# Two heads' score products queued as one run, and the merge's first products as one run behind the z projection, in a two-layer encoder

## The chip, the cores and the metric

The kernel runs on one core of one Trainium2 chip. The metric is device time in microseconds (us); lower is better.

## What is computed

Two layers over 256 tokens of width 1024. In each layer the normalised tokens `h` are projected once; the slices of the projection feed a gated delta rule with 8 heads (branch a) and a differential softmax attention with 8 heads (branch b). Cut to what matters here:

```python
proj = h @ w_in[l]
(q_a, k_a, v_a, ab_a, z_a, q_b, k_b, v_b, z_b, gate_a, gate_b) = jnp.split(proj, SPLIT_IDX, axis=-1)
y_a = gated_delta_branch(q_a, k_a, v_a, ab_a, z_a, ...)      # short convolutions, a triangular solve, chunks
s = jnp.einsum('nbhqd,nbhkd->nbhqk', q_blk, k)               # branch b: two score maps n for each head
p = jax.nn.softmax(s, axis=-1)
a = p[0] - lam * p[1]
o = jnp.einsum('bhqk,bhkd->bhqd', a, v)
y_b = rmsnorm(o, subln_w) * (1.0 - lambda_init) * jax.nn.silu(z_b)
merged = sigmoid(gate_a) * (y_a @ w_pa[l]) + sigmoid(gate_b) * (y_b @ w_pb[l])
x = x + merged @ w_out[l]
```

## The kernel before, in words

**Projections.** Each weight block of 1024 x 512 arrives in four loads of 256 rows (`raw`), and each load is split in two parts that together carry the float32 value: ScalarE writes `hi` (L230), VectorE writes `lo` (L232). A projection is then three products for each of the eight row blocks and each of the two token tiles m: hi by hi, lo by hi, hi by lo (L244 to L246). `hi` and `lo` have two buffers each, so the split of load kp+2 waits until the products of load kp have read it. In the program's names, `pp_zb000` and `pp_zb001` are the two accumulators (m = 0 and 1) of projection zb, layer 0, first half, and `lo_zb002` is the third load's low part of that projection; the first digit of a name is the layer, and for heads the second is the head. Order of the projections in a layer: k, v_b, q, q and k of branch b (`qk`), v, then zb (two halves), za (two halves), and the gates gb and ga around the merges with `w_pb` and `w_pa`.

**PSUM.** Eight banks: four under the tag `p` (two accumulators of the running projection and two more, which the score products of a head use), two under `c` (the turned blocks of the convolutions, `ctv` among them, and all products of the delta rule), two under `m` (turned blocks of q and k, `qkt`; a head's turned weights, `at`; its output, `av`).

**A head of branch b** (`head`, L829 to L871) is four score products on 64 of the 128 rows of the array each, for two query tiles and the two maps n = 1, 0 in turn (L839); then VectorE takes maxima (`mx`, L846), ScalarE exponentials (`es`, L848), VectorE the combination of the maps (`cc` L851 and L852, `es` L856), TensorE turns the result (`at`, L859), ScalarE copies it, TensorE multiplies by v (`av`, L865). Heads stand between the halves of the z projections in the program, and a scheduler orders the instructions of each engine: it takes them by their place in the program, as soon as it holds them ready and their buffers free by its own estimate of durations. Instructions written under `tc.high_priority` go ahead of others; `behind(x)` keeps an instruction after x on its engine; `keep_in_program_order` keeps a product behind the one written before it.

**What runs beside the heads.** VectorE solves the triangular systems of the delta rule by substitution: 31 steps of two instructions, `fstmp` (L670) and `X` (L671), each of which needs the one before it (`substitute(0, 31)`, written before the v convolutions). It also does the four taps of each block of the v convolution (`cvv`, L527), its SiLU (`thv`, L536), and the copy of the turned blocks out of PSUM (`vtm` from `ctv`, L547), and the rotary part of q and k (`r`, `stg`, L448 to L451). ScalarE has the tanh of the convolutions (L531), the exponentials, the splits and the PSUM copies.

**The merge of the solved blocks** (`merges`) begins with 64 products of 32 x 32 for each of two groups (`y64p`, L723). The first group's products may start behind row block 5 of the second half of za (`mark["done", 5]`), the second group's and the rest follow.

Of the kernel before, what the change touches and what calls it, by code (L numbers as in the profile page):

```python
# [17 lines left out]
P = 128  # L18
DM = 1024
KT = DM // P  # L20
SEQ = 256
NM = SEQ // P
# [6 lines left out]
HP = None  # L29
# [20 lines left out]
def hybrid_encoder(  # L50
# [19 lines left out]
    V, S, G, T = nc.vector, nc.scalar, nc.gpsimd, nc.tensor  # L70
# [18 lines left out]
    def banks2(name):  # L89
        return [ps_p.tile([P, 512], F32, tag="p", name=f"{name}{i}") for i in range(2)]  # L90

    def bank_c(name):
        return ps_c.tile([P, 512], F32, tag="c", name=name)
# [7 lines left out]
    mark = {}  # L101
# [102 lines left out]
    def behind(ins):  # L204
        return nullcontext() if ins is None else tc.issue_after(ins)
# [135 lines left out]
    for l in range(DEPTH):  # L341
# [139 lines left out]
        for m in range(NM):  # L481
            T.matmul(abq[:, m * 32 : (m + 1) * 32], abT[:, m * P : (m + 1) * P], id2,
                     start=True, stop=True)
# [213 lines left out]
        def merges(g):  # L697
# [17 lines left out]

            order = [(c, j4, mm, d) for c, j4 in every for mm in range(2) for d in range(2)]
            order.sort(key=lambda k: k != (0, 0, 1, 1))
            first = mark["done", 5] if g == 0 else None
            for n_, (c, j4, mm, d) in enumerate(order):
                b0, b1 = srcdst(d, mm)  # L720
                co = 32 * (b0 % 2)
# [104 lines left out]
        s_all = small.tile([P, NH, 2, NM], F32, tag="s_all", name=f"s_all{l}")  # L826
        ssb = small.tile([P, NM, NH], F32, tag="ssb", name=f"ssb{l}")
        ob = e4(f"ob{l}", "eo")
        def head(h):  # L829
            es = work.tile([P, 2, NM, SEQ], F32, tag="w4a", name=f"es{l}{h}", bufs=2)  # L830
            mx = small.tile([P, 2, NM], F32, tag="mx", name=f"mx{l}{h}")


            sp = banks2(f"sc{l}{h}")
            for qt in range(NM):
                for n in (1, 0):
                    rows = slice(64 * n, 64 * n + 64)
                    with nullcontext() if n else tc.high_priority(offset=HP):
                        mm = T.matmul(sp[n][:, qt * SEQ : (qt + 1) * SEQ],  # L839
                                      qkT[h // 4][rows, 0, h % 4, qt * P : (qt + 1) * P],  # L840
                                      qkT[h // 4][rows, 1, h % 4, :], start=True, stop=True)
                    if qt or not n:
                        tc.keep_in_program_order(mm)
            for n in range(2):
                spv = sp[n].rearrange("p (q k) -> p q k", q=NM)
                V.tensor_reduce(mx[:, n, :], spv, AX.X, ALU.max, negate=True)  # L846
# [69 lines left out]
        qk_part(1, 0)  # L916
        conv("v", C_VA, None, 1)
        qk_part(1, 1)
        head(0)
        z_part(zb, C_ZB, "zb", 0)  # L920
        head(1)
        z_part(zb, C_ZB, "zb", 1)
        head(2)
        head(3)
        z_part(za, C_ZA, "za", 0)
        mg = [merges(0), merges(1)]
        step(mg)
        step(mg)
        head(4)
        head(5)  # L930
        z_part(za, C_ZA, "za", 1)
        step(mg)
        head(6)
        with tc.high_priority(offset=HP):
            step(mg[:1])
        head(7)
# [141 lines left out]
```

## Time and profile before

| | |
|---|---|
| three runs | 779.36 to 779.75 us, median 779.53 |
| span of the profiled execution, first to last instruction | 777.1 us |
| what the median has beside that span | 2.4 us |
| TensorE busy | 758.2 us, 98% of the span |
| VectorE, ScalarE, GpSimd busy | 557.3, 474.9, 101.9 us |

The page gives the span of the profiled execution and no device time of its own, so the median stands for it; the 2.4 us lie before the first and behind the last instruction. In a timeline each row has the start, the time to the end of the last instruction in the row, the engine, the line, the operation, output and inputs (buffer numbers left out), and how many instructions are merged in the row. Float32 products outside the projections are two instructions each, so a head's four score products show as 8.

### The profile page before, as it was taken

How to read it: one execution, taken by the hardware profiler on the slowest of the kernel's cores; microseconds unless marked ns; L12 is line 12 of the kernel's file. 1: busy time of each engine (PE TensorE's matmuls, PEld its weight loads, DVE VectorE, ACT ScalarE, POOL GpSimd, SP SyncE). 2: the span in 40 equal slices, each digit the busy share in tenths (PEclk: the TensorE clock that was granted, in tenths of full speed). 3: DMA queues.
4: the chain of work that ended last, by engine and by line, in shares of the span. 5: the costliest groups of instructions: out<-in, count | busy, mean ns of one | idle time of the engine just before them, and what ended most of it. 6: DMA issues, size and time to landing. Idle time of an engine off the chain costs nothing.

```text
span 777.1 us, 13805 instructions
## 1 busy us (share of the span) xinstructions
PE 758.2 (98%) x5222; PEld 647.7 (83%) x5222; DVE 557.3 (72%) x1051; ACT 474.9 (61%) x1042; POOL 101.9 (13%) x137
## 2 busy tenths in 40 slices
PE   8999999999999999999999999999999999999996
PEld 4899879887778888887889888899777788888784
DVE  5686878999974635377677776989999553536782
ACT  5657776557677744564554668655577776356551
POOL 5100461100030100010010025510001110001000
PEclk9999999999999999999999999999999999999998
DMA  7752756554496644346664256755446954343631
GB/s 227 240 177 78 224 146 198 174 172 136 112 207 187 210 135 129 117 144 210 215 224 136 82 160 221 194 170 161 141 137 174 233 164 160 114 133 111 213 110 54
DMA packets 77745, 126.91 MB, mean 163 GB/s; under 512 B 19679, under 2 KB 20015, under 8 KB 77680
## 3 DMA queue, kind: packets, MB, share of 16 engines
q1 hardware_dynamic: 71038, 112.99, 48.4%
q0 software_dynamic: 3936, 9.77, 4.8%
q10 hardware_dynamic: 2706, 3.28, 1.3%
q8 instruction: 41, 0.67, 0.4%
q14 instruction: 24, 0.20, 0.1%
HBM read 121.27 MB, written 4.75 MB: 162 GB/s over the span
## 4 chain that ended last, share of the span: by engine, by line
PE 81%; DVE 7%; DMA 5%; ACT 4%; issue 2%; POOL 0%; SPq 0%; POOLq 0%; ACTq 0%; DVEq 0%
PE pp_vb L282 5%; DMA raw_q<-in_w_in_dram 3%; PE pp_qk L245 2%; PE pp_qk L246 2%; PE pp_qk L244 2%; PE pp_o L282 2%; PE pf_k L298 2%; PE pf_k L302 2%; PE pf_v L298 2%; PE pf_k L300 2%; PE pp_gb L245 2%; PE sc L839 2%; PE pp_gb L244 2%; PE pf_v L302 2%; PE pf_v L300 2%; PE av L865 2%
## 5 line engine op out<-in xcount | busy, mean ns | idle before, releaser
L245 PE MATMUL pp_qk<-lo_qk,hT 128*128 128x512 f32 x128 | 51.3, 401 | 1.0 <-DVE lo_qk L232 1.0
L246 PE MATMUL pp_qk<-hi_qk,hT 128*128 128x512 f32 x128 | 50.1, 391 | 0.0
L230 ACT CAST hi_qk<-raw_qk 128x1024 fp32r<-128x1024 f32 x32 | 33.5, 1046 | 23.6 <-PE pp_qk L246 12.6
L244 PE MATMUL pp_qk<-hi_qk,hT 128*128 128x512 f32 x128 | 46.1, 398 | 0.7 <-ACT hi_qk L230 0.7
L232 DVE TENSOR_TENSOR lo_qk<-raw_qk,hi_qk 128x1024 fp32r<-128x1024 f32 x32 | 40.2, 1257 | 7.6 <-ACT hi_qk L230 7.4
L232 DVE TENSOR_TENSOR lo_pb<-raw_pb,hi_pb 128x1024 fp32r<-128x1024 f32 x16 | 19.6, 1224 | 35.7 <-ACT hi_pb L230 35.7
L298 PE MATMUL pf_q<-hT,hi_q 128*128 128x256 f32 x128 | 36.5, 288 | 0.3 <-ACT hi_q L230 0.2
L298 PE MATMUL pf_v<-hT,hi_v 128*128 128x256 f32 x128 | 36.5, 289 | 0.0
L300 PE MATMUL pf_v<-hT,hi_v 128*128 128x256 f32 x128 | 36.2, 286 | 0.0
L300 PE MATMUL pf_q<-hT,hi_q 128*128 128x256 f32 x128 | 35.9, 284 | 0.0
L848 ACT ACTIVATE es<-sc,mx 128x256 f32<-128x256 f32 x64 | 29.8, 473 | 10.1 <-DVE mx L846 10.0
L298 PE MATMUL pf_k<-hT,hi_k 128*128 128x256 f32 x128 | 35.8, 285 | 0.0
L302 PE MATMUL pf_q<-hT,lo_q 128*128 128x256 f32 x128 | 35.7, 292 | 0.0
L300 PE MATMUL pf_k<-hT,hi_k 128*128 128x256 f32 x128 | 35.7, 283 | 0.0
L232 DVE TENSOR_TENSOR lo_gb<-raw_gb,hi_gb 128x1024 fp32r<-128x1024 f32 x16 | 19.6, 1224 | 22.2 <-ACT hi_gb L230 22.0
L232 DVE TENSOR_TENSOR lo_ga<-raw_ga,hi_ga 128x1024 fp32r<-128x1024 f32 x16 | 19.6, 1226 | 21.0 <-ACT hi_ga L230 21.0
L302 PE MATMUL pf_v<-hT,lo_v 128*128 128x256 f32 x128 | 34.6, 286 | 0.0
L302 PE MATMUL pf_k<-hT,lo_k 128*128 128x256 f32 x128 | 34.4, 285 | 0.0
L230 ACT CAST hi_pb<-raw_pb 128x1024 fp32r<-128x1024 f32 x16 | 16.8, 1049 | 25.1 <-PE pp_pb L246 24.3
L527 DVE SCALAR_TENSOR_TENSOR cvq<-pf_q,cw,cvq 128x254 f32<-128x254 f32 (+1 forms) x64 | 29.7, 476 | 1.8 <-ACT cvq L523 1.4
L527 DVE SCALAR_TENSOR_TENSOR cvv<-pf_v,cw,cvv 128x254 f32<-128x254 f32 (+1 forms) x64 | 30.2, 483 | 0.6 <-ACT cvv L523 0.5
L527 DVE SCALAR_TENSOR_TENSOR cvk<-pf_k,cw,cvk 128x254 f32<-128x254 f32 (+1 forms) x64 | 28.5, 478 | 2.0 <-ACT cvk L523 1.3
(356 smaller groups left out, 2495.5 us busy)
## 6 DMA issues: line engine op xcount, KB each, us to landing
raw_qk<-in_w_in_dram SPq DMA_DIRECT2D x32, 512.0 KB, 3.7
raw_k<-in_w_in_dram SPq DMA_DIRECT2D x16, 512.0 KB, 4.6
raw_q<-in_w_in_dram SPq DMA_DIRECT2D x16, 512.0 KB, 3.7
raw_v<-in_w_in_dram SPq DMA_DIRECT2D x16, 512.0 KB, 3.8
raw_zb<-in_w_in_dram SPq DMA_DIRECT2D x16, 512.0 KB, 3.6
raw_za<-in_w_in_dram SPq DMA_DIRECT2D x16, 512.0 KB, 3.7
raw_gb<-in_w_in_dram SPq DMA_DIRECT2D x16, 512.0 KB, 4.7
raw_o<-in_w_out_dram SPq DMA_DIRECT2D x16, 512.0 KB, 4.5
```

Of the source, the lines that this page charges most:

```text
L230: high = S.copy(hi[:, :, :n], raw[:, :, :n]).ins
L232: mark[nm, kp] = high, V.tensor_tensor(lo[:, :, :n], raw[:, :, :n], hi[:, :, :n].bitcast(F32), ALU.subtract).ins
L244: T.matmul(o, act[kt // 4][:, 0, kt % 4, ts_], hi, start=kt == 0, stop=False)
L245: T.matmul(o, act[kt // 4][:, 0, kt % 4, ts_], lo, start=False, stop=False)
L246: mark["proj"] = T.matmul(o, act[kt // 4][:, 1, kt % 4, ts_], hi, start=False, stop=kt == KT - 1).ins
L282: mark["proj"] = T.matmul(o, a_, w_, start=kt == 0 and a_ is ah and w_ is hi, stop=kt == KT - 1 and a_ is al).ins
L298: T.matmul(o, hi[:, cs], act[kt // 4][:, 0, kt % 4, :], start=first, stop=False, skip_group_check=True)
L300: T.matmul(o, hi[:, cs], act[kt // 4][:, 1, kt % 4, :], start=False, stop=False, skip_group_check=True)
L302: T.matmul(o, lo[:, cs], act[kt // 4][:, 0, kt % 4, :], start=False, stop=done, skip_group_check=True)
L527: V.scalar_tensor_tensor(ca[:, o0:o1], acc[:, b, o0 + sft : o1 + sft], cw[:, j, cb : cb + 1], ca[:, o0:o1], ALU.mult, ALU.add)
L839: mm = T.matmul(sp[n][:, qt * SEQ : (qt + 1) * SEQ], qkT[h // 4][rows, 0, h % 4, qt * P : (qt + 1) * P], qkT[h // 4][rows, 1, h % 4, :], s ...
L848: S.activation(es[:, n, qt, :], spv[:, qt, :], AF.Exp, bias=mx[:, n, qt : qt + 1], accum_out=s_all[:, h, n, qt : qt + 1])
```

## The change

`head` takes one or two heads. With two, the second head's scores go to the two banks of tag `c`, the first's to tag `p` as before; the second head's four products are written first, then the first head's, all kept in that order, and behind them the softmax and the rest of the first and then of the second (`attend`, unchanged). Heads 0 and 1 stand together ahead of the z projections (before: head 0 ahead of zb, head 1 between its halves); 2 and 3 together behind row block 3 of zb's second half, 4 and 5 together behind block 3 of za's first half, 6 alone behind block 2 of za's second half. Except for heads 0 and 1 and head 7, the first product is under high priority, which it was not before. In the merge the first group's products wait for row block 7, the last, instead of 5.

```diff
-            first = mark["done", 5] if g == 0 else None
+            first = mark["done", 7] if g == 0 else None
...
-        def head(h):
+        def head(*hs, after=None):
+            sps = [banks2(f"sc{l}{hs[0]}")] + [[bank_c(f"sc{l}{h}{i}") for i in range(2)] for h in hs[1:]]
+            lead = True
+            for h, sp in reversed(list(zip(hs, sps))):
+                for qt in range(NM):
+                    for n in (1, 0):
+                        rows = slice(64 * n, 64 * n + 64)
+                        with behind(mark["done", after] if lead and after is not None else None), \
+                                nullcontext() if lead and after is None else tc.high_priority(offset=HP):
+                            mm = T.matmul(sp[n][:, qt * SEQ : (qt + 1) * SEQ],
+                                          qkT[h // 4][rows, 0, h % 4, qt * P : (qt + 1) * P],
+                                          qkT[h // 4][rows, 1, h % 4, :], start=True, stop=True)
+                        if not lead:
+                            tc.keep_in_program_order(mm)
+                        lead = False
+            for h, sp in zip(hs, sps):
+                attend(h, sp)
...
-        head(0)
+        head(0, 1)
         z_part(zb, C_ZB, "zb", 0)
-        head(1)
         z_part(zb, C_ZB, "zb", 1)
-        head(2)
-        head(3)
+        head(2, 3, after=3)
         z_part(za, C_ZA, "za", 0)
         mg = [merges(0), merges(1)]
         step(mg)
         step(mg)
-        head(4)
-        head(5)
+        head(4, 5, after=3)
         z_part(za, C_ZA, "za", 1)
         step(mg)
-        head(6)
+        head(6, after=2)
```

**TensorE behind the last product of the `qk` projection, layer 0.** `qkt` are the last turned blocks of k, `ctv010` and `ctv012` the turned blocks of the v convolution in the two `c` banks, `sc01x` and `sc00x` the scores of heads 1 and 0. Before:

```order
L246 MATMUL pp_qk0111_1999<-hi_qk0113_2054,hT0_1_108 128x512
L839 MATMUL sc001_2101<-qkT0_0_281 128x256
L839 MATMUL sc000_2100<-qkT0_0_281 128x256
L839 MATMUL sc001_2101<-qkT0_0_281 128x256
L839 MATMUL sc000_2100<-qkT0_0_281 128x256
L244 MATMUL pp_zb000_2132<-hi_zb000_2134,hT0_0_107 128x512
```

And in the changed kernel, from the same product on:

```order
L246 MATMUL pp_qk0111_1999<-hi_qk0113_2054,hT0_1_108 128x512
L454 MATMUL qkt0011_2079<-ident_81,stg0110_2072 128x128 x4
L544 MATMUL ctv010_1968<-ident_81,thv011_1965 128x128 x2
L544 MATMUL ctv012_1992<-ident_81,thv012_1980 128x128 x2
L454 MATMUL qkt0111_2092<-ident_81,stg0111_2085 128x128 x4
L838 MATMUL sc011_2101<-qkT0_0_281 128x256
L544 MATMUL ctv012_1992<-ident_81,thv013_1989 128x128 x2
L838 MATMUL sc010_2100<-qkT0_0_281 128x256
```

Behind these stand the other six score products of the two heads, and then the first product of zb. Before, the `qkt` and `ctv` products of this list stood between the products of zb; the last of them, on `thv013`, stood behind all 48 products of zb's first half. Now all of them stand ahead of zb. The order is the same in layer 1.

**VectorE on the way to `thv013`**, the difference between before (-) and the changed kernel (+), layer 0:

```order
 L670 TENSOR_TENSOR fstmp0_347<-la0_344,X0_346 128x252
 L527 TENSOR_SCALAR cvv013_1983<-pf_v011_1829,cw0_268,cvv013_1983 128x255
-L852 TENSOR_SCALAR cc00_2112<-s_all0_348,neglam0_327,cc00_2112 128x2
 L671 TENSOR_TENSOR X0_346<-X0_346,fstmp0_347 128x14x18
-L232 TENSOR_TENSOR lo_zb002_2171<-raw_zb002_2172,hi_zb002_2170 128x1024
 L527 TENSOR_SCALAR cvv013_1983<-pf_v011_1829,cw0_268,cvv013_1983 128x255
-L856 TENSOR_SCALAR es00_2098<-es00_2098,cc00_2112 128x256 x2
 L670 TENSOR_TENSOR fstmp0_347<-la0_344,X0_346 128x255
-L232 TENSOR_TENSOR lo_zb003_2189<-raw_zb003_2190,hi_zb003_2188 128x1024
```

In the same stretch the two `mx00` and the other `cc00`, a little earlier, and `lo_zb010`, right ahead of `thv013`, also go: all of them now stand behind `thv013`, and the taps of the convolution and the substitution stay.

**VectorE behind the copy of `ctv012`**, changed kernel, layer 0:

```order
L547 TENSOR_TENSOR vtm0_331<-ctv012_1992,nrm0_334 128x2x2x128
L671 TENSOR_TENSOR X0_346<-X0_346,fstmp0_347 128x17x15
L670 TENSOR_TENSOR fstmp0_347<-la0_344,X0_346 128x252
L671 TENSOR_TENSOR X0_346<-X0_346,fstmp0_347 128x18x14
L670 TENSOR_TENSOR fstmp0_347<-la0_344,X0_346 128x247
L671 TENSOR_TENSOR X0_346<-X0_346,fstmp0_347 128x19x13
```

Seven more instructions of the substitution follow (twelve in all), then the maxima `mx00` and `mx01` of the two heads with single substitution instructions between them, `cc` and `es` of both heads in the same way, and only then `lo_zb002`. Before, maxima, combinations and low parts stood among the substitution one by one.

More of the change, by code (lines that the diff above doesn't have):

```diff
@@ L828, in hybrid_encoder, with attend @@
         ob = e4(f"ob{l}", "eo")
-        def head(h):
+        def head(*hs, after=None):
[15 more added lines that the diff above has]
+                attend(h, sp)
+        def attend(h, sp):
             es = work.tile([P, 2, NM, SEQ], F32, tag="w4a", name=f"es{l}{h}", bufs=2)
             mx = small.tile([P, 2, NM], F32, tag="mx", name=f"mx{l}{h}")
[L834 to L843, printed above, removed]
             for n in range(2):
```

## The prediction

> **What bounds the kernel now.** I read the page's busy times first, then a table by stretch: zb's first half in layer 0 and the same piece of layer 1.
>
> ```profile
> PE 758.2 (98%) x5222; PEld 647.7 (83%) x5222; DVE 557.3 (72%) x1051; ACT 474.9 (61%) x1042; POOL 101.9 (13%) x137
> 171.80:190.20 18.40, 17.95 (x90) 13.59 (x90) 17.89 (x43) 12.29 (x25) 0.00 (x0) 1.00 0.47 142
> 549.90:568.30 18.40, 17.91 (x91) 13.60 (x91) 17.89 (x43) 12.31 (x26) 0.00 (x0) 1.00 0.51 141
> ```
>
> The columns of the table are TensorE, its weight loads, VectorE, ScalarE and GpSimd busy, then the granted clock, the DMA share and GB/s. TensorE has work nearly all the time (98%): an idle microsecond of it is a microsecond of the end. But in this stretch VectorE is full as well, 17.89 of 18.40 us in either layer. So both keep pace only because their work lies side by side. What matters is which work TensorE still has while VectorE goes through taps, rotations and substitution.
>
> **First part: everything ahead of zb.** TensorE's timeline, before:
>
> ```profile
> 171.81 1.78 PE L839 MATMUL sc<-qkT 64*128 64x256 f32 x8
> 173.52 0.50 PE L244 MATMUL pp_zb<-hi_zb,hT 128*128 128x512 f32 x1
> ...
> 187.49 0.40 PE L245 MATMUL pp_zb<-lo_zb,hT 128*128 128x512 f32 x1
> 187.72 0.40 PE L246 MATMUL pp_zb<-hi_zb,hT 128*128 128x512 f32 x1
> ...
> 189.10 1.16 PE L865 MATMUL av<-vb,aT 128*128 128x128 f32 x8
> 190.10 0.38 PE L544 MATMUL ctv<-ident,thv 128*128 128x128 f32 x2
> 190.24 0.47 PE L244 MATMUL pp_zb<-hi_zb,hT 128*128 128x512 f32 x1
> ```
>
> zb's first half starts at 173.52, its second at 190.24; a product comes every 0.23 us (187.49, 187.72). In the changed kernel the last `ctv012` products, on `thv013`, stand ahead of zb. TensorE works in order, so nothing of zb starts before VectorE reaches `thv013`:
>
> ```profile
> 175.88 1.29 DVE L846 TENSOR_REDUCE mx<-sc 128x2 f32<-128x512 f32 x2
> 177.08 0.29 DVE L448 TENSOR_TENSOR r<-stg,sincos 128x128 f32<-128x128 f32 x1
> ...
> 178.54 0.69 DVE L547 TENSOR_TENSOR vtm<-ctv,nrm 128x512 f32<-128x512 f32 x1
> ...
> 180.65 1.23 DVE L232 TENSOR_TENSOR lo_zb<-raw_zb,hi_zb 128x1024 fp32r<-128x1024 f32 x1
> 181.78 0.49 DVE L527 SCALAR_TENSOR_TENSOR cvv<-pf_v,cw,cvv 128x255 f32<-128x255 f32 x1
> 182.17 0.89 DVE L856 SCALAR_TENSOR_TENSOR es<-es,cc 128x256 f32<-128x256 f32 x2
> 182.96 0.43 DVE L670 TENSOR_TENSOR fstmp<-la,X 128x255 f32<-128x255 f32 x1
> 183.30 1.23 DVE L232 TENSOR_TENSOR lo_zb<-raw_zb,hi_zb 128x1024 fp32r<-128x1024 f32 x1
> ...
> 185.29 0.43 DVE L670 TENSOR_TENSOR fstmp<-la,X 128x256 f32<-128x256 f32 x1
> 186.02 1.23 DVE L232 TENSOR_TENSOR lo_zb<-raw_zb,hi_zb 128x1024 fp32r<-128x1024 f32 x1 [0.30 <-ACT hi_zb L230]
> 187.16 0.42 DVE L536 SCALAR_TENSOR_TENSOR thv<-thv,cvv 128x256 f32<-128x256 f32 x1
> ```
>
> `thv013` is the last row, 187.16. By the changed order VectorE no longer does ahead of it: the two `mx` (175.88 to 177.08: 1.20), the two small `cc` (0.2), `lo` (180.65 to 181.78: 1.13), the two `es` (182.17 to 182.96: 0.79), `lo` again (1.13) and the third `lo` with its wait (from 185.72, the end of `fstmp`, to 187.16: 1.44). That is 5.9 us, so `thv013` starts at 181.3 and ends at 181.7. The `ctv012` products need 0.4. VectorE's copy `vtm` (0.69) then starts at 182.3, behind two substitution instructions, and ends at 183.0. Only then is the second `c` bank free for `sc010`; the first bank's copy stands ahead of the later taps and lets one score product through early. So of the run of eight, one comes alone and seven follow from 183.0. For their length:
>
> ```profile
> 195.57 0.39 PE L246 MATMUL pp_zb<-hi_zb,hT 128*128 128x512 f32 x1
> 195.89 1.13 PE L839 MATMUL sc<-qkT 64*128 64x256 f32 x8
> 196.96 0.73 PE L244 MATMUL pp_zb<-hi_zb,hT 128*128 128x512 f32 x2
> 197.53 0.60 PE L859 MATMUL at<-ident,es 128*128 128x128 f32 x4
> 196.43 0.60 PE L839 MATMUL sc<-qkT 64*128 64x256 f32 x4
> 196.65 0.38 PE L839 MATMUL sc<-qkT 64*128 64x256 f32 x2
> ```
>
> Four score products last 1.07 us (195.89 to 196.96); inside the run one more costs 0.22 (196.43 to 196.65, two instructions at once on the two halves of the rows). Seven cost 1.07 + 3 x 0.22 = 1.7, and **zb starts at 184.8 instead of 173.5**. Of these 11.3 us some 3 are work that TensorE did later before (8 `qkt`, 6 `ctv`, one head's scores); the others are waiting.
>
> The same rows price a run: from 195.57 to 197.53 there are three projection products (0.69) and four score products (0.87), together 1.56 of 1.96. So **entering and leaving costs 0.4 us**. That is what the change saves where a run goes.
>
> **Second part: zb's first half waits for VectorE again.** The first two loads' products, 24 x 0.23 = 5.5, end at 190.3. Then comes `at00`, which needs the softmax of head 0. Behind `vtm` VectorE has twelve substitution instructions in a row, each of which needs the one before:
>
> ```profile
> 195.99 0.41 DVE L671 TENSOR_TENSOR X<-X,fstmp 128x247 f32<-128x247 f32 x1
> 196.44 0.41 DVE L670 TENSOR_TENSOR fstmp<-la,X 128x240 f32<-128x240 f32 x1
> ```
>
> And the page's group of the exponentials:
>
> ```profile
> L848 ACT ACTIVATE es<-sc,mx 128x256 f32<-128x256 f32 x64 | 29.8, 473 | 10.1 <-DVE mx L846 10.0
> ```
>
> Alone on the engine, such a step takes 0.45 (195.99 to 196.44); among others it took 0.34 (182.96 to 183.30). Twelve take 5.2, from 182.9 to 188.1. Four maxima at 0.60 and two substitution steps bring 191.0, the small ones 191.7, the two `es` 192.5. ScalarE meanwhile has eight exponentials at 0.46 (29.8 / 64) from 188.7 to 192.4 and behind them the `hi` of load 2, until 193.5. VectorE has six small steps, the second head's `es`, and `lo_zb002` until 195.7. So `at00` starts at 192.2 instead of 190.3, and the third product of load 2, which reads `lo`, at 195.7 instead of 191.2: **4.5 us of waiting**. From there on the splits keep ahead. Ten products (2.3), two (0.5), `av00` (1.0, as from 189.10 to 190.10), `at01` (0.4, as from 197.53) and ten more (2.3) bring zb's second half to about 202.1. That is 11.9 later than 190.24, with `at01` (0.4) done beyond what before had done there: **11.4 us late**.
>
> **Third part: from there to the gates.** Heads 2 and 3 in one run save 0.4. But their eight exponentials now stand in one row on ScalarE ahead of `hi_za000`, and with `lo` the first products of za wait about 0.4. Still 11.4. Heads 4 and 5 in one run: -0.4; their row of exponentials ends while TensorE has 24 products of za, which hide it. The merge's first products:
>
> ```profile
> 232.39 0.61 PE L244 MATMUL pp_za<-hi_za,hT 128*128 128x512 f32 x2
> 232.93 0.31 PE L723 MATMUL y64p<-T,A 32*32 32x32 f32 x10
> 233.18 0.50 PE L245 MATMUL pp_za<-lo_za,hT 128*128 128x512 f32 x1
> 233.51 0.40 PE L246 MATMUL pp_za<-hi_za,hT 128*128 128x512 f32 x1
> ...
> 236.56 1.24 PE L723 MATMUL y64p<-T,A 32*32 32x32 f32 x118
> ```
>
> The first ten instructions took 1.12 - 3 x 0.23 = 0.43 between projection products; in the long run (118 in 1.17 to the next row) ten are 0.1. One run saves 0.33. Waiting for row block 7 costs nothing: behind the run stands `av06` (8 instructions, about 0.9), which covers ScalarE's copy of the result. The DMAs of the solved blocks move ahead of za's weight loads on SP's queue; since the substitution is done by about 199, they start early too, and the load behind them is read some 10 us later. I cost them at nothing; if that cover went, a late load would add its few microseconds at za.
>
> **Sum.** Per layer 11.4 - 0.4 - 0.3 = 10.7. Layer 1 has the same two orders, and its rows repeat those of layer 0 (the first score run at 549.9, the stretch as full). Behind the heads TensorE is again the bound and the number of its changes between kinds of products is that of before, so nothing is given back. 777.1 + 2 x 10.7 = 798.5 for the span, plus the 2.4 around it: **801 us**, against 779.5.
>
> **Rivals.**
>
> *The clock falls in the gaps.* At the end of the program:
>
> ```profile
> 768.00:770.00 2.00, 1.33 (x6) 0.75 (x4) 0.63 (x1) 0.00 (x0) 0.00 (x0) 1.00 0.70 262
> 770.00:772.00 2.00, 0.00 (x0) 0.00 (x0) 0.15 (x2) 0.82 (x3) 0.87 (x2) 0.86 0.00 0
> 772.00:774.00 2.00, 0.00 (x0) 0.00 (x0) 0.66 (x1) 0.62 (x1) 0.00 (x0) 0.50 0.23 87
> ```
>
> And near its start, where the turns of `h` stand twice:
>
> ```profile
> 6.95 1.97 PE L189 MATMUL pt_h<-ident,h_n 128*128 128x128 f32 x8
> 16.52 1.04 PE L189 MATMUL pt_h<-ident,h_n 128*128 128x128 f32 x8
> ```
>
> TensorE ends at 769.3, and the granted clock is 0.50 from about 771.4 (0.86 is 1.00 for 1.4 us and 0.50 for 0.6): two idle microseconds can do it, and my first gap has about 8 idle of 11.3 us, the second 4.5 of 5.4. The eight turns took twice as long at 7 us as at 16.5, so a slow start can last for up to some 7 us of work. After the first gap it is hidden, because `lo_zb002` comes at 195.7 in any case. After the second it is not: half speed for up to 7 us loses up to 3.5 us per layer, less the 0.4 that za waits anyway. I take half of the bound or more: 803.5 to 807. Against it: TensorE works on both sides of the second gap, and the clock may count that. [...]
>
> *Only the first gap is paid.* If VectorE gains as much in the second as the deferred low parts cost (it has no rope, taps or copies left there), 4.5 falls away per layer: 792. Against it speaks the count of 0.45 us steps, which the rows give.
>
> *No wait, only fewer runs: faster.* If `ctv012` and the copy behind it came within what TensorE has left to do, four runs per layer would go, three of scores at 0.4 and one at 0.3: 3 us in all, 776.5. It decides at 1.5 us of waiting per layer. For it stands the price of a run; against it, that between 171.8 and 183.0 TensorE has 2.5 us of products while VectorE has 11 us of its own in front.
>
> **How the numbers follow.** My forecast (797 to 803.5) has 0.57, the falling clock (to 807) 0.25, the first gap alone (790 to 797) 0.12, faster 0.04, near no change 0.02. The range 793 to 806.5 leaves out the faster cases, the ends of the clock's and of the gap's: about 2 in 10. A difference of 0.2% is about what a measurement of this kernel can tell from none. Faster 0.04, same 0.02, slower 0.94.
>
> **What would show it.** TensorE idle ahead of `qkt0011` and of the `ctv012` products, released by VectorE; zb's first product near 184.8 and the second half's near 202 in layer 0, and 378 us plus the delay later in layer 1; `at` and `lo_zb` as releasers in between; score runs of 16 instructions of about 2 us at heads 2, 3 and 4, 5. I am wrong if zb starts before 180, if the clock stands at 0.50 for long behind 190, or if a stage behind the heads loses or gains over 1 us.

## The result, and the profile after

The changed kernel takes **808.4 us** (median of 4 runs, 805.6 to 809.6) against 779.4 beside it: a ratio of 1.037, 95% interval 1.0357 to 1.0384. That is 29.0 us slower, where 21.5 were forecast (801, range 793 to 806.5). Sign, place and first wait were as forecast; 7.5 us more came from steps that the forecast had wrong, and they put the time above its range.

From the page after: TensorE's busy share and clock (40 slices, tenths), and the exponentials' group with ScalarE's idle time ahead of it, 26.9 us where it was 10.0:

```profile
PE 766.9 (95%) x5222; PEld 655.0 (81%) x5222; DVE 561.6 (70%) x1051; ACT 473.2 (59%) x1042; POOL 100.6 (12%) x137
...
PEclk9999999987999999999999999999799999999999
...
L854 ACT ACTIVATE es<-sc,mx 128x256 f32<-128x256 f32 x64 | 29.6, 484 | 26.9 <-DVE mx L852 26.9
```

Two tables by stretch answer to the prediction's first one. The first line is zb's start in the same 18.4 us behind the last `pp_qk` product: TensorE 11.8 us busy instead of 17.95, VectorE as full as before. The others follow the clock (the column behind GpSimd's): half from 176.7 to 186.9, full for 10.3 us, half again from 197.2 to 200.6.

```profile
172.22:190.62 18.40, 11.81 (x47) 7.77 (x45) 17.95 (x49) 5.66 (x14) 0.00 (x0) 0.72 0.22 63
```

```profile
176.70:186.90 10.20, 7.25 (x27) 4.48 (x26) 9.91 (x28) 1.86 (x4) 0.00 (x0) 0.50 0.15 50
186.90:197.20 10.30, 8.24 (x34) 5.68 (x34) 10.07 (x29) 6.13 (x19) 0.00 (x0) 1.00 0.01 2
197.20:200.60 3.40, 3.40 (x9) 2.64 (x9) 3.19 (x9) 0.00 (x0) 0.00 (x0) 0.50 0.71 169
```

To compare stages I count from the last `pp_qk` product of a layer. TensorE before, that product and the first ones of za, gb and the output:

```profile
171.43 0.39 PE L246 MATMUL pp_qk<-hi_qk,hT 128*128 128x512 f32 x1
...
205.44 0.47 PE L244 MATMUL pp_za<-hi_za,hT 128*128 128x512 f32 x1
...
242.09 0.50 PE L244 MATMUL pp_gb<-hi_gb,hT 128*128 128x512 f32 x1
...
368.10 0.39 PE L244 MATMUL pp_o<-hi_o,mT 128*128 128x512 f32 x1
```

The same engine after, with the waits between (in brackets: idle time ahead, and what ended it):

```profile
172.22 0.39 PE L246 MATMUL pp_qk<-hi_qk,hT 128*128 128x512 f32 x1
176.25 0.67 PE L454 MATMUL qkt<-ident,stg 128*128 128x128 f32 x4 [3.64 <-DVE stg L451]
...
182.44 0.69 PE L544 MATMUL ctv<-ident,thv 128*128 128x128 f32 x2 [1.63 <-DVE thv L536]
183.91 3.47 PE L838 MATMUL sc<-qkT 64*128 64x256 f32 x14 [0.78 <-DVE vtm L547]
187.31 0.50 PE L244 MATMUL pp_zb<-hi_zb,hT 128*128 128x512 f32 x1
...
196.68 0.50 PE L245 MATMUL pp_zb<-lo_zb,hT 128*128 128x512 f32 x1 [1.56 <-DVE lo_zb L232]
...
197.29 0.63 PE L245 MATMUL pp_zb<-lo_zb,hT 128*128 128x512 f32 x1
197.72 0.63 PE L246 MATMUL pp_zb<-hi_zb,hT 128*128 128x512 f32 x1
...
211.20 2.00 PE L838 MATMUL sc<-qkT 64*128 64x256 f32 x16
...
219.09 0.47 PE L244 MATMUL pp_za<-hi_za,hT 128*128 128x512 f32 x1
220.56 0.50 PE L245 MATMUL pp_za<-lo_za,hT 128*128 128x512 f32 x1 [0.76 <-DVE lo_za L232]
...
237.09 0.50 PE L245 MATMUL pp_za<-lo_za,hT 128*128 128x512 f32 x1 [0.45 <-DVE lo_za L232]
...
252.99 1.33 PE L723 MATMUL y64p<-T,A 32*32 32x32 f32 x128
...
257.69 0.28 PE L743 MATMUL z<-y,U__96 32*32 32x32 f32 x5 [1.20 <-issue]
...
258.30 0.47 PE L244 MATMUL pp_gb<-hi_gb,hT 128*128 128x512 f32 x1
...
382.16 0.62 PE L244 MATMUL pp_o<-hi_o,mT 128*128 128x512 f32 x2
```

In gains (-) and losses (+) against before, with layer 1 read from the same four products:

| stretch | forecast | layer 0 | layer 1 |
|---|---|---|---|
| last `pp_qk` to za's first product | 11.4 - 0.4 = +11.0 | 46.87 - 34.01 = +12.9 | +12.9 |
| za to gb | 0.4 - 0.4 - 0.3 = -0.3 | 39.21 - 36.65 = +2.6 | +3.8 |
| gb to the output | 0 | 123.86 - 126.01 = -2.2 | -1.1 |
| sum | 10.7 | 13.3 | 15.5 |

The profiled execution is the slowest of the four and has 1.9 us more ahead of these stretches, 0.8 at the start and 1.1 at layer 1's q.

### The profile page after: what moved, and what is told of

It reads as the page before. It is cut to its first block, busy times and chain, and to the rows that moved or that the text cites. A ratio compares the mean times of both kernels' runs of the same rounds, so it can differ in the third digit from the quotient of the medians.

```text
span 807.7 us, 13781 instructions
## 1 busy us (share of the span) xinstructions
PE 766.9 (95%) x5222; PEld 655.0 (81%) x5222; DVE 561.6 (70%) x1051; ACT 473.2 (59%) x1042; POOL 100.6 (12%) x137
## 4 chain that ended last, share of the span: by engine, by line
PE 76%; DVE 12%; ACT 5%; DMA 3%; issue 3%; POOL 0%; SPq 0%; POOLq 0%; ACTq 0%; DVEq 0%
PE pp_vb L282 5%; PE pp_qk L245 3%; PE pp_qk L246 2%; PE pp_qk L244 2%; PE pp_o L282 2%; PE pf_v L298 2%; PE pp_gb L244 2%; PE pp_gb L245 2%; PE pp_gb L246 2%; PE pf_v L302 2%; PE pf_v L300 2%; PE pp_pb L245 2%; PE pp_pb L244 2%; PE pp_pb L246 2%; PE pp_ga L246 2%
## 5 line engine op out<-in xcount | busy, mean ns | idle before, releaser
L854 ACT ACTIVATE es<-sc,mx 128x256 f32<-128x256 f32 x64 | 29.6, 484 | 26.9 <-DVE mx L852 26.9
```

Of the source, the lines that this page charges most:

```text
L854: S.activation(es[:, n, qt, :], spv[:, qt, :], AF.Exp, bias=mx[:, n, qt : qt + 1], accum_out=s_all[:, h, n, qt : qt + 1])
```

## The experiments

My theory after the result had four parts, a rival to each: (1) the pair of heads 0 and 1 carries the loss, not the runs behind it; (2) the half clock behind the second gap costs 1.5 us per layer, not only the waiting; (3) the pairs 2, 3 and 4, 5 lose by ScalarE's row of exponentials; (4) the merge's one run brings the `issue` stalls, idle time of TensorE in which it waited for nothing that the profile shows. Times are medians; ratios go against the kernel before, timed on the same chip.

| kernel | us | ratio, 95% interval |
|---|---|---|
| heads 0, 1 apart | 784.8 | 1.0072 (1.0049 to 1.0096) |
| heads 0, 1 paired, nothing else | 805.5 | 1.0327 (1.0304 to 1.0349) |
| pairs 2, 3 and 4, 5 alone | 785.2 | 1.0063 (1.0042 to 1.0085) |
| gaps filled | 801.4 | 1.0272 (1.0247 to 1.0297) |
| second gap filled | 805.4 | 1.0335 (1.0308 to 1.0361) |
| substitution late | 802.8 | 1.0297 (1.0270 to 1.0325) |
| substitution late, first gap filled | 799.0 | 1.0242 (1.0222 to 1.0262) |
| pair 0, 1 behind zb's first block | 793.3 | 1.0171 (1.0153 to 1.0190) |
| pairs alone, second softmax held | 780.3 | 1.0012 (1.0002 to 1.0022) |
| merge's run alone | 780.1 | 1.0013 (0.9999 to 1.0027) |
| change without the merge's run | 806.4 | 1.0341 (1.0317 to 1.0364) |
| merge twice, in pieces | 778.8 | 0.9994 (0.9979 to 1.0010) |
| merge twice, in one run | 778.1 | 0.9981 (0.9968 to 0.9994) |
| pair 4, 5 and head 6 | 779.1 | 0.9989 (0.9979 to 1.0000) |
| the same with the merge's run | 785.2 | 1.0073 (1.0047 to 1.0099) |
| pair 4, 5 held, and head 6 | **777.5** | **0.9973 (0.9958 to 0.9988)** |

**Which part costs what.** Three kernels put parts of the change back.

```diff
 heads 0, 1 apart
-        head(0, 1)
+        head(0)
         z_part(zb, C_ZB, "zb", 0)
+        head(1)
 pair 0, 1 alone
-        head(2, 3, after=3)
+        head(2)
+        head(3)
 (4, 5 and 6 alike, and mark["done", 5] as before)
 pairs alone: heads 0, 1 apart, and mark["done", 5]
```

> All of the change except the pair of heads 0 and 1, whose scores are queued one head at a time as before. Theory A (the two gaps behind that pair carry the whole loss, the other runs save what a run costs): 779.4 - 2 x (0.4 + 0.4 + 0.3) = 777, no idle TensorE ahead of qkt0011, clock 1.00 throughout. Rival B (part of the loss comes from the later runs: the waits of za's products for lo_za of 0.76 and 0.45 us per layer and the issue stalls of 1.2 and 2.3 us in the merge stay): 781 to 785.

> The pair of heads 0 and 1 alone; heads 2 to 6 and the merge's first products as before. Theory A (this pair is the whole loss): the time of the changed kernel plus the 2 us that the other runs save, about 810, with zb's first product some 13 us late and both half-clock stretches in each layer. Rival B (the later runs cost 2 to 3 us per layer): 802 to 805.

> The pairs 2, 3 and 4, 5 at their given places; heads 0 and 1 as before, and the merge's first products released at the same row block as before. Against the kernel with only heads 0 and 1 apart it tells what the merge's one run does. Theory A (one run saves 0.33 us per layer): this kernel is 0.7 us slower than that one, about 778. Rival B (one run of 128 small products right ahead of the two runs behind it outruns the supply of instructions, and TensorE stands 1 to 2 us per layer without a releaser): this kernel is 1 to 3 us faster than that one, and no such stall stands in it.

The pair 0, 1 alone costs 26.0 us, 13.0 per layer, and the rest of the change 3.0 on top of it; by itself the rest costs 5.3. Rival B holds in the first and, within 0.5 us of its range, in the second. Part (1) of the theory falls: the pair carries most of the loss, but the runs that were to save 2 us lose too. The pairs alone lose 5.7 us already, so the merge's run adds nothing on average between these two, in spite of its stalls: with it `heads 0, 1 apart` stood 1.53 us without a releaser in layer 0 and 3.43 in layer 1; without it there was none over 0.1 us.

In the kernel with the pair alone `lo_zb002` comes 24.4 us behind `pp_qk`, as in the changed kernel (24.5), but in its profiled execution no half clock followed the second gap, in either layer. The stretch of 3.4 us that holds layer 0's gap (such stretches are counted from the changes of the clock, see the last section) began 0.5 us earlier in the layer there and had 61% of TensorE's time busy, where the changed kernel had 43%:

```profile
193.10:196.52 3.42, 2.08 (x12) 1.43 (x10) 3.42 (x11) 2.51 (x4) 0.00 (x0) 1.00 0.02 5
```

za is as late there all the same (47.2 us): the scores of heads 2 and 3 come in four pieces of 3.4 us together, where the changed kernel has one run of 1.9. So its 26.0 us are not the forecast's 22.8 and a half clock.

**The clock.** Products that nothing reads fill TensorE's idle time; each writes a bank that the following product overwrites.

```diff
+    def fill(ps, n, act, ins=None):
+        for _ in range(n):
+            with behind(ins):
+                T.matmul(ps, act[0][:, 0, 0, 0:P],
+                         act[0][:, 0, 0:2, :].rearrange("p a b -> p (a b)"), start=True, stop=True)
 gaps filled: 14 ahead of qkt0011, 6 ahead of the ctv012 products on thv013, 6 ahead of at00
 second gap filled: 7 behind at00
```

> The changed kernel with idle stretches of TensorE filled by products that nothing reads: 14 ahead of qkt0011, 6 ahead of the ctv013 products, 6 ahead of at00, 0.23 us each, 6.0 us in all per layer, inside waits that last longer. Theory A (half clock in and behind the gaps costs some 1.7 us in the score run, hidden, and 1.6 us behind the second gap, not hidden): granted clock at 1.00 through both gaps, seven score products 1.7 us instead of 3.4, zb's first product 1.7 us earlier, its second half 1.6 to 2 us earlier, 804 to 805.5. Rival B (waiting alone, the clock costs nothing on the path): 808, the second gap longer by what the first saves. Rival C (the fillers push the turns behind them): above 809.

> The changed kernel with 7 products that nothing reads (0.23 us each, 1.6 in all) behind the at00 turns, inside the second gap; the first gap stays as it is, and the order of VectorE and ScalarE up to za in layer 0 is that of the changed kernel. It parts the clock from the waiting behind the second gap. Theory A (8 products at half speed behind the gap cost 1.6 us per layer): granted clock 1.00 from 197 to 201, the products behind lo_zb002 0.23 apart, zb's second half 1.6 us earlier in layer 0; 805 to 806 in all. Rival B (the half speed was hidden in a later wait): the products full speed, but za's first product and the time (808) as before. Rival C (7 products are too few to keep the clock): the products still 0.43 apart, 808.

TensorE with the gaps filled, layer 0:

```profile
183.18 1.99 PE L846 MATMUL sc<-qkT 64*128 64x256 f32 x14 [0.96 <-DVE vtm L555]
185.10 0.50 PE L250 MATMUL pp_zb<-hi_zb,hT 128*128 128x512 f32 x1
...
195.94 0.70 PE L251 MATMUL pp_zb<-lo_zb,hT 128*128 128x512 f32 x1 [1.56 <-DVE lo_zb L238]
196.44 0.63 PE L252 MATMUL pp_zb<-hi_zb,hT 128*128 128x512 f32 x1
196.87 0.63 PE L251 MATMUL pp_zb<-lo_zb,hT 128*128 128x512 f32 x1
```

The score run takes 1.92 us instead of 3.4, so half clock had doubled it; zb starts 1.6 us earlier in its layer. But `lo_zb` comes when it came before, and za starts 46.8 us behind `pp_qk`, as in the changed kernel (46.9): the first gap's half clock was hidden, as the prediction says. Behind the second gap the products still come 0.43 apart. So in layer 0 rival B holds. The 7 us that this kernel gained came in layer 1, where the new schedule put fewer substitution steps ahead of `lo_zb` and za started at 42.2. Two things changed there at once, so this run does not part them; it is a hint at VectorE's order.

The second kernel is the clean one: VectorE keeps its order up to za, and ScalarE too but for one cast in layer 1. The stretch of 3.41 us that holds the second gap, filled, and the one behind it:

```profile
195.65:199.06 3.41, 2.83 (x13) 1.99 (x12) 3.31 (x11) 1.66 (x3) 0.00 (x0) 1.00 0.03 5
199.06:202.47 3.41, 3.41 (x23) 3.04 (x22) 3.24 (x8) 1.34 (x2) 0.30 (x1) 1.00 0.80 187
```

and the stretch of the gap in the changed kernel (busy 1.47 of 3.40 us, then half clock):

```profile
193.80:197.20 3.40, 1.47 (x6) 0.78 (x5) 3.33 (x11) 1.97 (x3) 0.00 (x0) 1.00 0.03 5
```

With the clock at 1.00 za starts 45.5 us behind `pp_qk` instead of 46.9, in layer 1 45.3 instead of 46.9: **where it comes, the half clock behind the second gap costs 1.5 us per layer**, theory A. The whole is 3.0 us faster by the medians; the two intervals just overlap.

**VectorE's queue in the second gap.**

```diff
-        substitute(0, 31)
-        spread_blocks()
+        substitute(0, 15)
 ...
         head(0, 1)
+        with tc.issue_after(mark["es"]):    # the last es of head 1
+            substitute(15, 31)
+        spread_blocks()
```

> The changed kernel with the substitution's steps from column 15 on queued on VectorE behind the softmax of heads 0 and 1 instead of ahead of it. Theory A (the second gap is VectorE's queue of substitution steps ahead of the maxima and of lo_zb002): the wait for lo_zb002 and the half-clock stretch behind it go, the first gap and its half clock stay; per layer 3 us of waiting and 1.6 us of clock less: 798 to 800. Rival B (ScalarE's exponentials and hi_zb002, or the load of the weights, are late anyway): lo_zb002 at most 1 us earlier, 806 to 808. Rival C (the deferred steps come back as lateness of the splits of zb's second half or of the merge): the wait moves there, 804 to 808.

> The kernel with the late substitution, with 14 unread products ahead of qkt0011 and 6 ahead of the ctv013 products besides, so that the first gap keeps the clock too. Theory A (the first gap's half clock, 1.5 us on the score run, was hidden in the changed kernel only by the wait for lo_zb002; with that wait gone it lies open): zb's first product 1.5 us earlier than in the late substitution kernel and its second half too, 798.5 to 800.5. Rival B (zb then waits for the softmax instead): 802 to 803.

TensorE with the late substitution alone, then with the first gap filled too:

```profile
183.09 3.78 PE L838 MATMUL sc<-qkT 64*128 64x256 f32 x14 [0.78 <-DVE vtm L547]
...
193.91 0.50 PE L245 MATMUL pp_zb<-lo_zb,hT 128*128 128x512 f32 x1 [0.24 <-DVE lo_zb L232]
```

```profile
185.57 1.99 PE L846 MATMUL sc<-qkT 64*128 64x256 f32 x14 [0.78 <-DVE vtm L555]
...
195.03 0.50 PE L251 MATMUL pp_zb<-lo_zb,hT 128*128 128x512 f32 x1 [0.90 <-DVE lo_zb L238]
```

The wait for `lo_zb` falls from 1.56 to 0.24 us and za starts at 43.9 instead of 46.9 (in layer 1 at 44.3), so the second gap was VectorE's queue of substitution steps. Of these 3.0 us a part comes back between za and gb (40.8 us instead of 39.2 in layer 0). The wait goes as theory A has it, part of it comes back as in C, and 802.8 lies between their ranges. With that wait gone, the first gap's half clock lies open: filling it brings another 1.6 us at za (42.3), and 3.8 us in all.

**The pair behind zb's first block.**

```diff
-        head(0, 1)
         z_part(zb, C_ZB, "zb", 0)
+        head(0, 1, after=1)
```

> The changed kernel with the pair of heads 0 and 1 behind the first row block of zb's first half instead of ahead of zb: TensorE starts zb at once, and the turns, the ctv products and the scores come in where VectorE is ready for them. Theory A (the loss of this pair is only that zb stands behind the wait): no idle TensorE of over 1 us ahead of qkt0011 or ctv013, clock 1.00, and what stays is the loss of the other pairs, 783 to 787. Rival B (the softmax of both heads comes so late that zb's second half waits for it in its place): 790 to 800.

```profile
186.69 0.44 PE L544 MATMUL ctv<-ident,thv 128*128 128x128 f32 x2 [1.40 <-DVE thv L536]
189.69 2.08 PE L838 MATMUL sc<-qkT 64*128 64x256 f32 x8 [2.57 <-DVE vtm L547]
```

The time, 793.3, lies in B's range, but not for B's reason: TensorE waits for `thv` and `vtm` here, not for the softmax, and A's "no idle TensorE of over 1 us" fails as well. zb starts 0.4 us behind `pp_qk`, and 8.1 of the 12.9 us at za are gone (38.7 behind `pp_qk`). Of the 4.7 us that stay at za, 4.0 are these two waits. The longer stands ahead of the run because the second head's scores need the `c` bank that the `ctv012` copy frees; half clock follows it (0.50 from 189.6 to 192.6 us).

**The pairs 2, 3 and 4, 5.** ScalarE in the kernel with the pairs alone, around za's second half:

```profile
213.53 1.04 ACT L230 CAST hi_za<-raw_za 128x1024 fp32r<-128x1024 f32 x1 [1.18 <-PE pp_za L246]
217.46 0.48 ACT L854 ACTIVATE es<-sc,mx 128x256 f32<-128x256 f32 x1 [2.89 <-DVE mx L852]
...
221.62 1.09 ACT L230 CAST hi_za<-raw_za 128x1024 fp32r<-128x1024 f32 x1
```

and TensorE behind it:

```profile
222.77 0.73 PE L244 MATMUL pp_za<-hi_za,hT 128*128 128x512 f32 x2 [0.34 <-ACT hi_za L230]
224.34 0.50 PE L245 MATMUL pp_za<-lo_za,hT 128*128 128x512 f32 x1 [0.84 <-DVE lo_za L232]
```

ScalarE stands 2.89 us ahead of the first of eight exponentials, since their maxima come late, and `hi_za` is queued behind all eight. A kernel that keeps the runs but holds the second head's softmax of each pair behind the next half's first split:

```diff
-            for h, sp in zip(hs, sps):
-                attend(h, sp)
+            attend(hs[0], sps[0])
+            return [lambda late, h=h, sp=sp: attend(h, sp, late) for h, sp in zip(hs[1:], sps[1:])]
 ...
-        head(4, 5, after=3)
+        rest = head(4, 5, after=3)     # 2, 3 alike
         z_part(za, C_ZA, "za", 1)
+        rest[0](mark[f"za{l}1", 0])    # maxima behind lo_za, exponentials behind hi_za
         step(mg)
-        head(6, after=2)
+        head(6)
```

> The kernel with the pairs 2, 3 and 4, 5 alone, in which the second head's maxima and exponentials of each pair wait until the first load of the following half of za is split. The scores still go in one run. Theory A (the pairs lose 2.2 us per layer because ScalarE stands ready for eight exponentials in a row, 2.9 us idle for the maxima, while hi_za is queued behind them): the waits of 0.99 and 0.34 + 0.84 us for za's splits go, and 785.2 becomes 780 to 781.5. Rival B (the loss is something else of the pairs, as the turns and av products that now stand alone): waits gone, time at 784 to 786. Rival C (the held softmax comes late and za waits for its banks or the merge for its scores): new waits, 782 or more.

Its ScalarE at the same place:

```profile
216.72 0.49 ACT L856 ACTIVATE es<-sc,mx 128x256 f32<-128x256 f32 x1
...
217.93 1.03 ACT L230 CAST hi_za<-raw_za 128x1024 fp32r<-128x1024 f32 x1
```

The cast comes 3.7 us earlier, behind four exponentials, and TensorE no longer waits for za's splits: 780.3 instead of 785.2, theory A. This kernel also has head 6 at its place of before. That can't be what took away the 2.17 us of waiting that both layers had, since these waits stood ahead of head 6's scores; 0.91 us more, in layer 1 alone, stood behind them and may be head 6's. The runs themselves, though, save nothing that shows: 1.0012 (1.0002 to 1.0022).

**The merge's run.**

```diff
 alone, in the kernel before
-            first = mark["done", 5] if g == 0 else None
+            first = mark["done", 7] if g == 0 else None
 twice (products issued a second time, with 5 and with 7)
-            for n_, (c, j4, mm, d) in enumerate(order):
+            for n_, (c, j4, mm, d) in enumerate(order * (2 if g == 0 else 1)):
 change without it: mark["done", 5] in the changed kernel
```

> The kernel before with one edit: the merge's first products wait for row block 7 instead of 5, so that 128 of them go in one run behind za. Nothing else moves. Theory A (a run between projection products costs 0.33 us, one run saves it): 779.4 - 0.7 = 778.7. Rival B (the run outruns the supply of instructions; stalls without a releaser, as those of 1.2 to 3.4 us in the kernels that have it): 780 to 785, such stalls on the zt and z products in both layers, and a spread of over 2 us between runs.

> The changed kernel with the merge's first products released at row block 5 as before, so that they stand in four pieces between za's products; head 7's scores then fall behind them, and the turns of at07 into gb's products as before. Theory A (the one run of 128 brings stalls without a releaser on the zt and z products, 1.2 us in layer 0 and 2.3 us with half clock behind it in layer 1, and the spread of the changed kernel's runs): no such stall, 804 to 806 and a spread under 2 us. Rival B (the earlier place of heads 6 and 7 that comes with the run makes pa 1.8 us per layer shorter, which pays for the stalls): stalls gone, but pa's products take 23.6 us again instead of 21.9, 807 to 809.

> The kernel before with the merge's first products of one half issued twice (64 more instruction records of 10 ns per layer), released at row block 5 as before, so they stand in pieces. It is the control for the next run. Theory A (instructions come at a limited rate; spread over more time they keep up): +0.6 us per layer for the added work, 780 to 781, issue stalls no longer than the 0.6 us of before. Rival B (stalls come with the number of instructions alone): stalls over 1 us here too.

> As the one before, with the products released at row block 7, so that all of them go in one run right ahead of the zt and z products. Theory A (the run outruns the supply): the stalls on zt and z grow from the 0 and 1.35 us of the kernel with the run alone to over 2 us per layer, 783 to 787 and a wide spread. Rival B (the stalls have to do with something else, as the place of heads 6 and 7): stalls under 1.4 us, 780 to 781.5.

Alone the run gains nothing (forecast -0.7): za is 0.5 us shorter in each layer, but `av06` behind the run then waits for ScalarE's copy, 1.45 us in layer 0 and 0.64 in layer 1, a wait that before does not have, and layer 1 has a stall of 1.35 us. In the changed kernel the run costs 2.0 us by the medians, with intervals that overlap, and both theories of that run are right in part: without it the stalls are gone, but gb to the output takes 126.0 us again instead of 123.9 (layer 0), and pa within it 25.0 instead of 22.7. The spread stays: 3.8 us without the run's stalls, where theory A had under 2. The run of the doubled products, 192 in one piece, had no `issue` stall over 0.1 us, so length alone is not the cause, and a limited supply of instructions, theory A of both, is not shown:

```profile
236.39 1.90 PE L723 MATMUL y64p<-T,A 32*32 32x32 f32 x192
```

As a control this pair was poor: both kernels also drew the turns of head 7 forward and got the shorter pa, and layer 0 of the second waits 0.80 and 0.55 us for head 7 behind the run. But the stalls answer to something else. Here is layer 0's in the kernels with the gaps filled, the second gap filled, and substitution late with the first gap filled, each with the number of `z` products still to do behind the stall (x):

```profile
257.18 0.86 PE L751 MATMUL z<-y,U__96 32*32 32x32 f32 x31 [1.82 <-issue]
```

```profile
258.66 0.38 PE L749 MATMUL z<-y,U__96 32*32 32x32 f32 x12 [1.29 <-issue]
```

```profile
255.23 0.60 PE L751 MATMUL z<-y,U__96 32*32 32x32 f32 x26 [1.54 <-issue]
```

These kernels have 26, 7 and 20 added products ahead of it, the changed kernel none and 5 `z` products left: 5 + 26 = 31, 5 + 7 = 12, 5 + 20 = 25 (26 seen). **The stall keeps its place in TensorE's stream of instructions while the program moves under it.** Counted in TensorE's products, the changed kernel stands still at the 1621st (layer 0, 1.20 us) and the 4164th (layer 1, 2.28 us), and before at the 4154th (layer 1, 0.63 us). Not every stall fits: one of 1.58 us, in the pair 4, 5 with head 6 and the merge's run, stands at none of these places. What makes such a place, no run shows.

The traces also tell when it costs. In the changed kernel TensorE took the 128 products ahead of the two places in 2.6 and 2.5 us. In the kernel before they took 4.6 us ahead of the 1621st product, where it stood for no more than 0.1 us, and 4.0 ahead of the 4154th. In layer 0 they took 4.0 without the merge's run, which had no stall; the 192 products of the other kernel lie farther ahead, and its last 128 took 4.6. So of these places TensorE stood for over 1 us at the two with 128 products in 2.6 us or less ahead of them, and for 0.63 us at most where they took 4.0 or more. No kernel was built to try this by itself.

**Versions meant to beat both.** Heads 0 to 3 as before, the pair 4, 5 and head 6 placed (`six_45`); the same with the merge's run; the same without it but with the softmax of head 5 held as above.

> A version meant to beat both: heads 0 to 3 and the merge as before, only the pair 4, 5 and head 6 at their given places. Theory A (the pair 0, 1 and the row of exponentials of 2, 3 are the losses; the earlier place of heads 6 and 7 makes pa 1.8 us per layer shorter; the pair 4, 5 saves 0.4 and waits 1.2): 779.4 - 2 x (1.8 + 0.4 - 1.2) = 777.4. Rival B (the earlier heads take as much from gb and the splits as pa gains): 779 to 781.

> As the kernel with the pair 4, 5 and head 6 placed, with the merge's first products in one run behind row block 7. Theory A (one run saves 0.33 per layer and costs stalls of 1 to 3 us on the zt and z products): 778 to 781 and a spread of 2 us or more. Rival B (the run is a gain once heads 6 and 7 are out of its way): 776 to 777, no stall over 0.6 us.

> A version meant to beat both: heads 0 to 3 and the merge as before, the scores of 4 and 5 in one run with the second softmax held behind the first split of za's second half, head 6 at its given place. Theory A: as the kernel with the pair 4, 5 and head 6 placed (779.1), less its 0.9 us wait for lo_za per layer: 777.0 to 777.8. Rival B (the softmax held back moves heads 6 and 7 back, and with them what pa gained): 779 to 780.5.

The first cannot be told from before; the merge's run adds 6 us to it, with stalls of 1.58, 1.17 and 2.87 us, which neither theory had. The last is **1.9 us faster than before**, as theory A has it, and against the first its wait of 0.9 us per layer is gone. Its gain over before is not that of the run: za's end stands at 64.9 us behind `pp_qk`, before at 64.8. Nor is it simply pa. pa takes 22.7 us instead of 25.0, since before the turns and splits of ya stand right ahead of its first products, which wait for them (0.74 us in each layer), for instance here:

```profile
351.20 0.50 PE L245 MATMUL pp_pa<-lo_pa,yaT 128*128 128x512 f32 x1 [0.53 <-DVE lo_pa L232]
```

But gb and pb are 2.9 us longer, because work has moved into them. Layer 0 gained nothing in the profiled executions, which differ by 1.0 us. In layer 1 the stretch from za's end to gb became 1.8 us shorter (4.5 instead of 6.2); before has a stall there, and this kernel none:

```profile
619.51 0.59 PE L737 MATMUL zt<-U__96,y 32*32 32x32 f32 x47 [0.63 <-issue]
```

So the cause of the 1.9 us is not shown: one trace of each is too little for it.

## Why the prediction was wrong, point by point

- **What bounds the kernel: right.** Between `qk` and za TensorE waits for VectorE. Filling the waits ahead of zb and of `at00` with products that nothing reads changed nothing at za in layer 0 (46.8 us); putting VectorE's substitution off brought 3.0.
- **First part: right where it counts.** `thv013` was forecast at 181.3 and the `ctv012` products behind it came at 181.7 in the time of before (182.44 less the 0.8 that this run was late). zb started at 186.5, not 184.8: the seven score products took 3.4 us, not 1.7, at half clock. As said in the first rival, `lo_zb002` hides this; the third product of load 2 came at 195.9, forecast 195.7.
- **Second part: the step that failed is "ten products (2.3)" behind the gap.** They took 4.0 us (196.68 to 200.66), since eight of them came 0.43 apart, at half clock. za was 1.5 us per layer later for it, 3 us in all. The falling clock stood as a rival with a chance of 0.25; its bound was 3.5 per layer. Against it I had put that TensorE works on both sides of the gap. It fell all the same behind a stretch with 1.47 of 3.40 us busy; the kernel with the pair alone had the same gap in a stretch with 2.08 of 3.42 us busy and kept its clock.
- **Third part: failed in sign.** "Their row of exponentials ends while TensorE has 24 products of za, which hide it": ScalarE first waits for VectorE's maxima, 2.9 us in the kernel with the pairs alone, which I left out, and za then waits for its splits: 1.2 us per layer in the changed kernel, where I had 0.4. "Waiting for row block 7 costs nothing": it brought stalls of 1.2 and 2.3 us, where before has one of 0.6, which I took for nothing. Forecast were -1.4 us for all of the third part; measured, the changed kernel less the pair 0, 1 alone, +3.0.
- **"The run saves 0.4": too high.** TensorE's score rows over heads 0 to 7 in layer 0, before and with the two pairs alone:

```profile
171.43:242.09 70.66, 10.40 (x64) 6.08 (x64) 10.62 (x16) 15.69 (x63) 1.00 0.63 162
```

```profile
171.50:244.70 73.20, 9.85 (x64) 6.24 (x64) 10.27 (x16) 15.31 (x63) 1.00 0.63 158
```

  10.40 to 9.85: two runs fewer save 0.55 in these rows, not 0.8. The price of 0.4 was read between two projection products; three of the four runs before have turns behind them, and these have to be entered in any case.
- **"Nothing is given back": failed.** Heads 6 and 7 moved forward, and gb to the output became 2.2 us (layer 0) and 1.1 us (layer 1) shorter. pa, which no longer waited, went from 25.0 to 22.7 us and ga from 32.8 to 29.0, while gb and pb took up work and grew.

Together, by the stretches of the table and both layers: 3.8 us more than forecast up to za, of which the half clock is 3.0; 7.0 more from za to gb, of which the waits of za's splits are 1.6 and the stalls 2.7; 3.3 less behind gb. That is 7.5, where the forecast fell 7.6 short of the medians. The loss from za to gb and the gain behind it were both unforeseen, and that they cancel in part is luck. What stays open: the rest of the 7.0, and the spread of 4 us between runs of the changed kernel, which does not go with the stalls.

## What to carry to other kernels

Joining small products into one run was worth about 0.3 us a run here (0.55 for two score runs); count first what the run must wait for, and every queue in which its consumers then stand in a row (here ScalarE's cast `hi_za` behind eight exponentials, the first at 217.46, the cast at 221.62 us). Where a gap opens, price the half clock behind it (1.5 us per layer here) unless a later wait covers it, and look at the busy share of the stretch around the gap (43% with half clock behind it, 61% without) rather than at the gap alone. To keep a joined run, hold the second consumer behind the work that the next stage needs.

## What the runs showed of the hardware

- A stretch of 3.4 us in which TensorE was 43% busy, with no idle time over 1.6 us, was followed by 3.4 us at half clock; one that was 83% busy (second gap filled) was not.
- Half clock comes in stretches of 10.2 us and 3.4 us here. In the trace of the changed kernel the changes of the granted clock lie whole multiples of 3.41 us apart (3, 3, 1, 108, 3, 3, 1, 17, 1 and 44 of them). In the 3.41 us ahead of its six falls to 0.50 TensorE was busy for 0.45, 1.48, 0.56, 1.48, 1.14 and 0.00 us by the profile's rows. Of the other such stretches at full clock the emptiest, from 797.93 and from 16.28 us, had 2.04 and 2.09 us busy, and the clock stayed at 1.00 behind them. The kernel before has one fall, at its end, behind 1.30 us busy of 3.41.
- In the changed kernel TensorE stood still, waiting for nothing that the profile shows, inside rows of 32 x 32 products (128 of them in 1.26 us in the merge's run): for 1.20 us at its 1621st product and for 2.28 us at its 4164th; with heads 0, 1 apart for up to 3.4 us. Seven products added some 60 us earlier moved layer 0's stall by seven products.
